# Eight PSUM banks dealt out anew in a two-layer hybrid block: separate rings for attention's maxima and scores, one bank for its value sums

## The chip, the cores and the metric

The kernel runs on one core of one Trainium2 chip, in one launch. The time is device microseconds; the time before is the median of three runs. A profile of one more execution, and its trace, stand beside it. A core has five engines that each run their own queue in order: TensorE (PE, matmuls; its weight loads are shown as PEld), VectorE (DVE), ScalarE (ACT), GpSimd (POOL) and SyncE (SP, which here issues nearly all DMAs). Matmuls write into PSUM; here all eight banks of 2 KB for each of the 128 partitions are given to the kernel's pools, and one bank holds one tile of 128 x 512 f32.

## The reference

Two layers over 1024 latent tokens and 256 context tokens, width 1024. In each layer a modulated rms norm feeds one wide input projection; its columns go to three branches, and their outputs are joined by an output projection that is added to the stream.

```python
for i in range(DEPTH):                                   # 2
    h, h_c = modulate(x, ...), modulate(ctx, ...)
    z, xbc, dtr, q, k, v, ga, ua, ub, gc = split_cols(h @ w_in[i])      # and for h_c
    ssd_lat  = ssd_branch(z, xbc, dtr, ...)              # conv of 5, chunked scan, 12 heads
    ql, kl   = rope(rmsnorm(q)), rope(rmsnorm(k))        # 12 query heads, 4 key heads, 64 wide
    attn_lat = attend(ql, concat(kl, kc), concat(vl, vc)) * silu(ga)    # softmax over 1280 keys
    conv_lat = conformer_branch(ua, ub, gc, ...)         # depthwise conv of 31, layernorm, matmul
    x = x + gate * (concat(ssd_lat, attn_lat, conv_lat) @ w_out[i])
    ...                                                  # the context likewise, in layer 0 only
return rmsnorm(x, final_norm_g)
```

## The kernel before, in words

All is f32. Products that need it are made of three fp32r matmuls on a split into a high and a low part (`mm3`). Each layer has three stages.

**Projections (`phase_b`).** For each of 10 tiles of 128 tokens, or for strips of 512 or 256 tokens, a group of 24 matmuls fills one PSUM tile of the pool `pm` (tag `m`); ACT or DVE reads it (`chain`, `gate`, `fm_fin`). Beside these groups DVE runs the depthwise convolutions (`conv_cm` into `cac`, `conv_x` into `xcv`), `conv_x` transposes its result on PE in three pieces of up to four tiles (`px`, `pt`, `px`; the copies are called `xsg`), and `cm_tail` transposes `cac` into a tile of `pt`, from which DVE takes the statistics and writes `xn`, which is transposed again into `px`.

**Attention (`attn`) with the scan (`ssd`) beside it.** A unit is a pair of query heads with 256 queries; there are 30 in layer 0 (24 large ones over 10 key tiles, 6 small ones over 2) and 24 large ones in layer 1. For a unit, `maxima` multiplies queries by keys in pieces of 512, 512 and 256 keys (12 matmuls, `m<-k_a,q_a` in the profile), DVE reduces each piece to a row maximum (`a_sm`, line 935), and the negated maxima go through a tile of `pv` into a row of the query operand. `scores` then makes for each key tile a transposed score tile (`m<-q_a,k_a` and `m<-q_b,k_b`), from which ACT takes the exponential (`a_p`), and DVE or POOL add the tiles up (`a_ac`, `a_a`). `values` multiplies `a_p` by the values into the first half of a tile of `pt` (`t<-a_p,vs`), in a block of four key tiles and one of six; `finish` puts the column sums into the second half of that tile (`t<-a_a,twos`), DVE takes their reciprocal (line 1011) and multiplies it by the first half (line 1012), and POOL applies the gate. Maxima run two units ahead of scores. The value block of a unit is emitted after the `finish` of the unit before it. `ssd` uses `px`.

**Output projection (`out_half`).** For each token tile and column half two groups (`pa`, `pb`) in `pm`, read by ACT and DVE.

The order on each engine is not written out by hand: `at(us)` gives what follows a due time, and a planner takes, of what is ready by its own estimate of durations and has a free PSUM or SBUF slot, what is due first. That order, and which tile gets which bank, is then fixed; on the chip every engine goes through its queue in order and waits where a bank is not yet read out. So a change of the pools can change the order everywhere.

The pools of PSUM before: `pm` 4 banks (all projection groups, maxima and scores), `pt` 2 (value accumulators, transposes, the modulation vectors of `ada`), `pv` 1 (transposes of queries and keys, the row of maxima, the small matmul of `cm_tail`), `px` 1.

Of the kernel before, what the change touches and what calls it, by code (L numbers as in the profile page):

```python
# [13 lines left out]
PSUM = bass.MemoryType.PSUM  # L14
DRAM = bass.MemoryType.DRAM

DEPTH = 2
PM = 4
PT_ = 2
PX_ = 1  # L20
CM_PACE = 1.7
TAIL = 40.0
# [138 lines left out]
def build(tc, a, out, depth=DEPTH, dump=None):  # L161
    nc = tc.nc
    es = ExitStack()
    V, S, G, P, Y = nc.vector, nc.scalar, nc.gpsimd, nc.tensor, nc.sync

    def at(us):
        tc.cur_priority = int(us * 100)

    def pool(st, name, bufs=1, **k):
        return st.enter_context(tc.tile_pool(name=name, bufs=bufs, **k))  # L170
# [3 lines left out]
    def mk(p, shape, tag, dt=F32, bufs=None):  # L174
        uid[0] += 1
        k = {} if bufs is None else {"bufs": bufs}
        return p.tile(shape, dt, tag=tag, name=f"{tag}_{uid[0]}", **k)

    cp = pool(es, "cp")
    dp = pool(es, "dp", space=DRAM)  # L180
    pm = pool(es, "pm", PM, space=PSUM)
    pt = pool(es, "pt", PT_, space=PSUM)
    pv_ = pool(es, "pv", 1, space=PSUM)
    px = pool(es, "px", PX_, space=PSUM)

    def dr(shape, name, dt=F32):
        t = dp.tile(shape, dt, tag=name, name=name)
        if dump is not None:
            dump[name] = t
        return t  # L190

    def mm(o, l, r, start, stop):
        P.matmul(o, l, r, start=start, stop=stop)  # L193

    def tr(o, i, idt):
        P.transpose(o, i, idt)  # L196

    def act(o, i, f, **k):
        S.activation(o, i, f, **k)  # L199
# [33 lines left out]
    for l in range(depth):  # L233
        t = mk(cp, [128, NCOL], f"colc{l}")
        Y.dma_start(out=t, in_=a["colc"][l])
        colc.append(t)
        t = mk(cp, [128, NROW], f"rowc{l}")
# [80 lines left out]
    def norm_tile(l, t, h, wp):  # L318
        r = 0 if t < 8 else 1
        xt = mk(wp, [128, DM], "n_x", bufs=3 if l == 0 else 1)  # L320
        if l == 0:
            Y.dma_start(out=xt, in_=a["xin"][t])
        else:
            for n in range(2):
                Y.dma_start(out=xt[:, 512 * n:512 * n + 512], in_=x_d[t][n])
        hh, hl = h
        tok = slice(t * 128, t * 128 + 128)
        hf = mk(wp, [128, KT, 128], "n_h", bufs=2 if l == 0 else 1)
        ss = mk(wp, [128, 4], "n_ss", bufs=4)
        act(hl[:, :, tok], xt.rearrange("p (k t) -> p k t", k=KT), AF.Square, accum_out=ss[:, 0:1])  # L330
        rs_pow(ss[:, 2:3], ss[:, 0:1], 1.0 / DM, ss[:, 1:2], 1)
        act(xt, xt, AF.Copy, scale=ss[:, 2:3])
        for f4 in range(2):
            ps = mk(*((pt, [128, 4, 128], "t") if f4 else (px, [128, 4, 128], "x")))
            for i in range(4):
                f = 4 * f4 + i
                tr(ps[:, i, :], xt[:, f * 128:(f + 1) * 128], idf)
            for i in range(4):
                f = 4 * f4 + i
                s1, s2 = msc[l][:, f, r:r + 1], msh[l][:, f, r:r + 1]  # L340
                if f4:
                    ts(V, hf[:, f, :], ps[:, i], s1, ALU.mult, s2, ALU.add)
                else:
                    act(hf[:, f, :], ps[:, i], AF.Identity, scale=s1, bias=s2)
        V.tensor_copy(hh[:, :, tok], hf)
        (V if t % 2 else G).tensor_tensor(hl[:, :, tok], hf, hh[:, :, tok].bitcast(F32), ALU.subtract)
# [87 lines left out]
    def phase_b(l, nh, b0, pp):  # L434
# [50 lines left out]

        def tm(i, n, j, t, w):
            nn = 280 if n == "q" and j == 2 else 256
            ps = mk(pm, [128, 512], "m")
            mm3(ps[:, 0:nn], lambda x, k: h[x][:, k, t * 128:t * 128 + 128], lambda x, k: w[x][:, k, :], KT)
            if n == "k":  # L490
                chain(ps, "k", t, k_d[t])
            elif n == "v":
                o = mk(qp, [128, 256], "c_v", bufs=2)
                act(o, ps[:, 0:256], AF.Copy)
                Y.dma_start(out=v_d[t], in_=o)
            else:
                if j == 2:
                    V.tensor_copy(dtr[:, t, :], ps[:, 256:280])
                if t < nq:
                    chain(ps, "q", t, q_d[j][t])  # L500
# [56 lines left out]
        def conv_x(j, t0):  # L557
            xp = xps[j]
            at(t0)
            o = mk(xp_p, [128, 1282], "xcv", bufs=2)  # L560
            w = sw[:, 5 * j:5 * j + 5]
            ts(V, o, xp[:, 0:1282], w[:, 0:1], ALU.mult, sw[:, 50 + j:51 + j], ALU.add)
            for k in range(1, 5):
                at(t0 + 2 * k)
                stt(o, xp[:, k:k + 1282], w[:, k:k + 1], o, ALU.mult, ALU.add)
            at(t0 + 10)
            th = mk(up_p, [128, 1282], "th")
            act(th, o, AF.Tanh)
            stt(o, th, 1.0, o, ALU.add, ALU.mult)
            if j >= 6:  # L570
                d = bT_d[j - 6] if j < 8 else cT_d[j - 8]
                Y.dma_start(out=d[:, 0:1024], in_=o[:, 0:1024])
                Y.dma_start(out=d[:, 1024:1280], in_=o[:, 1026:1282])
            if j < 8:
                at(t0 + XLAG)
                sg = mk(gp, [128, NT, 128], "xsg")
                for ta in (0, 4, 8):
                    n = min(4, NT - ta)
                    ps = mk(*((pt, [128, 4, 128], "t") if ta == 4 else (px, [128, 4, 128], "x")))
                    for t in range(ta, ta + n):  # L580
                        c0 = t * 128 + (2 if t >= 8 else 0)
                        tr(ps[:, t - ta, :], o[:, c0:c0 + 128], idf)
                    act(sg[:, ta:ta + n, :], ps[:, 0:n, :], AF.Copy)
                if j < 6:
                    d = xt_d[:, :, 128 * j:128 * j + 128]
                else:
                    d = bt_d[:, :, 128 * (j - 6):128 * (j - 6) + 128]
                Y.dma_start(out=d.rearrange("t p f -> p t f"), in_=sg)
# [34 lines left out]
        def block(i):  # L623
            u = FM_UNITS[i]
            u0 = b2 + 26 * i
            at(u0 - 20)
            w = wblock(wt, wt, a["wfm"][l, i], "wt", 2)
            tt = u0
            for m, (n, j) in enumerate(u):
                full = n == "xbc" or not last  # L630
                for t0, tn in ((0, 512), (512, 512), (1024, 256)):
                    if t0 >= 1024 and not full:
                        continue
                    at(tt)
                    ps = mk(pm, [128, 512], "m")
                    mm3(ps[:, 0:tn], lambda x, k: w[x][:, k, 128 * m:128 * m + 128],
                        lambda x, k: h[x][:, k, t0:t0 + tn], KT)
                    fm_fin(ps, n, j, t0, tn)
                    tt += 5.2 * tn / 512
                if n == "ua":  # L640
                    conv_cm(j, tt, CM_PACE)
                if n == "xbc":
                    conv_x(j, tt)
# [260 lines left out]
    def attn(l, ap, c0, pre):  # L904
# [18 lines left out]
        def maxima(i):  # L923
            qa, qb = qst[i]
            pcs = [(0, 512), (512, 512), (1024, 256)] if units[i][1] < 4 else [(1024, 256)]
            n = len(pcs)
            sm = mk(ap, [128, 4, 3], "a_sm", bufs=1)
            nm = mk(ap, [128, 4], "a_nm", F32R, bufs=2)
            for x in range(2):
                ka = kst[kv(i, x)][0].rearrange("p t k -> p (t k)")  # L930
                for t in range(2):
                    for j, (k0, kn) in enumerate(pcs):
                        ps = mk(pm, [128, 512], "m")
                        mm(ps[:, 0:kn], qa[:, x, t, :], ka[:, k0:k0 + kn], True, True)
                        V.tensor_reduce(sm[:, 2 * x + t, j:j + 1], ps[:, 0:kn], axis=AX.X, op=ALU.max)  # L935
                        yield
            V.tensor_reduce(nm, sm[:, :, 0:n], axis=AX.X, op=ALU.max, negate=True)
            ps = mk(pv_, [128, 4, 128], "v")
            for j in range(4):
                mm(ps[0:65, j, :], nm[:, j:j + 1].to_broadcast([128, 65]), idr, True, True)  # L940
            act(qb[64:65], ps[64:65].rearrange("p (x t) q -> p x t q", x=2), AF.Copy)
            yield
# [138 lines left out]
    def out_half(l, n, yp, wp, w, d0, fin):  # L1081
# [9 lines left out]
        for t in range(nq):  # L1091
# [12 lines left out]
            r = 0 if t < 8 else 1  # L1104
            xt = mk(yp, [128, 512], "ox", bufs=nb)
            Y.dma_start(out=xt, in_=a["xin"][t][:, s] if l == 0 else x_d[t][n])
            pa = mk(pm, [128, 512], "m")
            nk, k0, yy = pcs[0]
            mm3(pa, lambda x, k: yy[x][:, k, :], lambda x, k: w[k0 + k][x], nk)
            pb = mk(pm, [128, 512], "m")  # L1110
            for i, (nk, k0, yy) in enumerate(pcs[1:]):
                mm3(pb, lambda x, k: yy[x][:, k, :], lambda x, k: w[k0 + k][x], nk, i == 0, i == 1)
            t1 = mk(wp, [128, 512], "wor") if nb == 1 else mk(yp, [128, 512], "ot", bufs=2)
# [95 lines left out]
```

## Time and profile before

| | |
|---|---|
| median of 3 runs | 2922.65 us (2918.71 to 2924.61) |
| the profiled execution | 2926.13 us; its span, from the first to the last instruction, 2924.1 us |
| busy, share of the span | PE 2714.5 us (93%), PEld 2111.4 (72%), DVE 2175.7 (74%), ACT 1062.2 (36%), POOL 1165.6 (40%) |
| granted TensorE clock, mean | 0.965 |

In the groups of instructions a name such as `m<-k_a,q_a` says which tile is written from which. In rows of groups the figures are the number of instructions, the busy time in us and the mean of one in ns, and behind the bar the idle time of the engine just before them with what ended it. Rows of waits give the waiting engine and tile, what it waited for, us in total, how often, and the longest. Rows of the timeline give the start, the length, the engine and the instruction, with `x` for how many in a row are merged; a merged row's length runs over all of them.

### The profile page before, as it was taken

To read this page: it belongs to the slowest core of one execution; us is meant where nothing else is said; L and a number is where in the kernel's file an instruction comes from. 1 tells how busy PE (TensorE), PEld (TensorE's weight loads), DVE (VectorE), ACT (ScalarE), POOL (GpSimd) and SP (SyncE) were. 2 spreads that over 40 slices of the span, in tenths; PEclk is the share of its full clock that TensorE was granted. 3 is DMA by queue.
4 is the path that set the end of the run, shared out by engine and by line. 5 is a ranking of instruction groups with operands and counts; after the bars stand their busy time and mean duration, and the time that the engine had idled before them with its cause. 6 is when DMAs were issued, how large, how long until landed. Compare 5 with 4: busy or idle time off the path is not lost. (4 is left out here: it accounts for less than half of the span.)

```text
span 2924.1 us, 41057 instructions
## 1 busy us (share of the span) xinstructions
PE 2714.5 (93%) x15708; PEld 2111.4 (72%) x15708; DVE 2175.7 (74%) x2987; ACT 1062.2 (36%) x1801; POOL 1165.6 (40%) x832
## 2 busy tenths in 40 slices
PE   5999998999998888999999999999998998999998
PEld 3888876888856655666787998877886665666676
DVE  4476899973299989797445587999835989898644
ACT  4212221222245454454335222222224454644432
POOL 2244122232168677571112352222323667675111
PEclk9999998999999989899999999999999999999999
DMA  6551111223343222224645322113234232312554
GB/s 237 191 159 66 56 55 65 90 98 105 115 137 108 73 88 84 74 68 130 205 147 162 114 76 67 55 63 107 102 127 151 73 98 72 103 59 62 164 152 143
DMA packets 284035, 314.44 MB, mean 108 GB/s; under 512 B 27606, under 2 KB 219190, under 8 KB 282814
## 3 DMA queue, kind: packets, MB, share of 16 engines
q1 hardware_dynamic: 283838, 311.82, 33.5%
q8 instruction: 123, 2.02, 0.3%
q14 instruction: 74, 0.61, 0.1%
HBM read 236.25 MB, written 75.50 MB: 107 GB/s over the span
## 5 line engine op out<-in xcount | busy, mean ns | idle before, releaser
L193 PE MATMUL m<-hh,wth 128*128 128x512 f32 (+1 forms) x1440 | 533.7, 371 | 0.1
L193 PE MATMUL m<-hl,wth 128*128 128x512 f32 (+1 forms) x1440 | 532.2, 370 | 0.0
L193 PE MATMUL m<-hh,wtl 128*128 128x512 f32 (+1 forms) x1440 | 531.6, 369 | 0.0
L199 ACT ACTIVATE a_p<-m 128x512 f32<-128x512 f32 x492 | 285.5, 596 | 373.1 <-PE m L193 362.7
L208 DVE SCALAR_TENSOR_TENSOR cac<-up,cmw,cac 128x1295 f32<-128x1295 f32 (+1 forms) x240 | 383.2, 1617 | 1.9
L935 DVE TENSOR_REDUCE a_sm<-m 128x1 f32<-128x512 f32 (+1 forms) x600 | 331.0, 583 | 52.8 <-PE m L193 50.2
L359 POOL TENSOR_TENSOR wtl<-wr,wth 128x1024 fp32r<-128x1024 f32 x68 | 201.9, 2969 | 404.2 <-ACT wth L199 404.1
L193 PEld LDWEIGHTS m<-hh,wth 128*128 128x128 f32 x1440 | 273.0, 190 | 47.8 <-ACT th L199 0.5
L193 PEld LDWEIGHTS m<-hh,wtl 128*128 128x128 f32 x1440 | 272.5, 189 | 48.1
L193 PEld LDWEIGHTS m<-hl,wth 128*128 128x128 f32 x1440 | 272.7, 189 | 47.3
L193 PE MATMUL m<-q_a,k_a 128*128 128x512 f32 (+1 forms) x656 | 255.3, 399 | 23.1 <-ACT a_p L199 10.9
L193 PE MATMUL m<-k_a,q_a 128*128 128x512 f32 (+1 forms) x600 | 242.0, 440 | 24.9 <-DVE a_sm L935 19.3
L193 PE MATMUL t<-a_p,vs 128*64 128x256 f32 x1968 | 250.9, 397 | 0.9 <-ACT a_p L199 0.4
L193 PE MATMUL m<-woh,yl 128*128 128x512 f32 x576 | 227.7, 397 | 6.1 <-DVE yl L1101 5.9
L193 PE MATMUL m<-woh,yh 128*128 128x512 f32 x576 | 226.6, 396 | 5.2 <-ACT yh L199 5.2
L193 PE MATMUL m<-wol,yh 128*128 128x512 f32 x576 | 226.6, 395 | 0.8 <-DVE wol L1077 0.8
L193 PE MATMUL m<-q_b,k_b 65*128 65x512 f32 (+1 forms) x656 | 223.1, 350 | 0.0
L193 PEld LDWEIGHTS t<-a_p,vs 128*64 128x64 f32 x1968 | 138.7, 142 | 89.1 <-issue 17.2
L193 PEld LDWEIGHTS m<-q_a,k_a 128*128 128x128 f32 x656 | 129.3, 197 | 84.3 <-ACT a_p L199 23.4
L193 PEld LDWEIGHTS m<-k_a,q_a 128*128 128x128 f32 x600 | 117.0, 201 | 99.6 <-DVE a_sm L935 38.2
L199 ACT ACTIVATE wth<-wr 128x1024 fp32r<-128x1024 f32 (+1 forms) x84 | 89.3, 1063 | 255.6 <-DMA wr<-in_wfm 136.2
L193 PE MATMUL m<-wth,hh 128*128 128x256 f32 (+1 forms) x608 | 173.6, 288 | 1.3 <-ACT wth L199 0.8
(239 smaller groups left out, 5629.5 us busy)
## 6 DMA issues: line engine op xcount, KB each, us to landing
wr<-in_wfm SPq DMA_DIRECT2D x68, 512.0 KB, 3.6
s_cb<-cum_d SPq DMA_DIRECT2D x72, 384.0 KB, 3.7
ada_w<-in_adaw SPq DMA_DIRECT2D x32, 512.0 KB, 4.6
wor<-in_wout SPq DMA_DIRECT2D x64, 256.0 KB, 3.1
s_x<-xt_d SPq DMA_DIRECT2D x38, 384.0 KB, 3.2
yf<-ys_d SPq DMA_DIRECT2D x36, 384.0 KB, 3.9
yf<-ya_d SPq DMA_DIRECT2D x36, 384.0 KB, 4.2
yf<-yc_d SPq DMA_DIRECT2D x36, 256.0 KB, 2.9
```

The source lines that it names most:

```text
L193: P.matmul(o, l, r, start=start, stop=stop)
L199: S.activation(o, i, f, **k)
L208: V.scalar_tensor_tensor(o, i, s, i1, op0, op1)
L359: (e or G).tensor_tensor(lo[:, s], raw, hi[:, s].bitcast(F32), ALU.subtract)
L935: V.tensor_reduce(sm[:, 2 * x + t, j:j + 1], ps[:, 0:kn], axis=AX.X, op=ALU.max)
```

## The change

The eight banks are given out anew. `pm` has two banks and is used in attention by `scores` alone; a new pool `pn` (tag `n`) has three and is used in attention by `maxima`; the groups of the projections and of the output take the five in turn (`gemm`: n, n, m, n, m). `pt` has one bank instead of two, so a unit's value accumulator and the next unit's share it. In `norm_tile` the second half of the transposes goes to `pt` for odd tiles and to `pv` for even ones, and in `conv_x` the third piece goes to `pv` instead of to `px` again.

```diff
-PM = 4
-PT_ = 2
+PM = 2
+PN = 3
+PT_ = 1
...
     pm = pool(es, "pm", PM, space=PSUM)
+    pn = pool(es, "pn", PN, space=PSUM)
...
+    turn = [0]
+
+    def gemm():
+        turn[0] += 1
+        return mk(pm, [128, 512], "m") if turn[0] % 5 in (0, 3) else mk(pn, [128, 512], "n")
...                                          # norm_tile
-            ps = mk(*((pt, [128, 4, 128], "t") if f4 else (px, [128, 4, 128], "x")))
+            ps = mk(*((pt if t % 2 else pv_, [128, 4, 128], "t" if t % 2 else "v") if f4 else (px, [128, 4, 128], "x")))
...                                          # tm and block of phase_b, pa and pb of out_half
-            ps = mk(pm, [128, 512], "m")
+            ps = gemm()
...                                          # conv_x
-                    ps = mk(*((pt, [128, 4, 128], "t") if ta == 4 else (px, [128, 4, 128], "x")))
+                    ps = mk(*((pt, [128, 4, 128], "t") if ta == 4 else (px if ta == 0 else pv_, [128, 4, 128], "x" if ta == 0 else "v")))
...                                          # maxima
-                        ps = mk(pm, [128, 512], "m")
+                        ps = mk(pn, [128, 512], "n")
```

No instruction is added or left out: the same matmuls, reductions, copies and DMAs remain.

More of the change, by code (lines that the diff above doesn't have):

```diff
@@ L634, in block @@
                     at(tt)
-                    ps = mk(pm, [128, 512], "m")
+                    ps = gemm()
                     mm3(ps[:, 0:tn], lambda x, k: w[x][:, k, 128 * m:128 * m + 128],
@@ L932, in maxima @@
                     for j, (k0, kn) in enumerate(pcs):
-                        ps = mk(pm, [128, 512], "m")
+                        ps = mk(pn, [128, 512], "n")
                         mm(ps[:, 0:kn], qa[:, x, t, :], ka[:, k0:k0 + kn], True, True)
@@ L1106, in out_half @@
             Y.dma_start(out=xt, in_=a["xin"][t][:, s] if l == 0 else x_d[t][n])
-            pa = mk(pm, [128, 512], "m")
+            pa = gemm()
             nk, k0, yy = pcs[0]
             mm3(pa, lambda x, k: yy[x][:, k, :], lambda x, k: w[k0 + k][x], nk)
-            pb = mk(pm, [128, 512], "m")
+            pb = gemm()
             for i, (nk, k0, yy) in enumerate(pcs[1:]):
```

## The prediction

> **What bounds the kernel now.** I read the page's first lines, then the busy times by stage (the four stretches below are attention of layer 0 and of layer 1, then the projections of layer 0 and of layer 1), then PE's waits in each stretch.
>
> ```profile
> span 2924.1 us, 41057 instructions
> PE 2714.5 (93%) x15708; PEld 2111.4 (72%) x15708; DVE 2175.7 (74%) x2987; ACT 1062.2 (36%) x1801; POOL 1165.6 (40%) x832
> ...
> 820.00:1380.00 560.00, 504.41 (x3336) 342.16 (x3335) 493.71 (x683) 284.35 (x488) 359.31 (x216) 0.94 0.29 88
> 2225.00:2740.00 515.00, 471.13 (x3041) 317.82 (x3040) 452.03 (x636) 262.37 (x451) 316.95 (x189) 0.95 0.30 91
> 200.00:820.00 620.00, 587.29 (x3167) 500.86 (x3166) 454.45 (x492) 141.73 (x228) 170.59 (x137) 0.97 0.26 85
> 1700.00:2225.00 525.00, 507.80 (x2575) 426.19 (x2573) 406.23 (x459) 124.95 (x193) 151.25 (x121) 0.99 0.27 88
> ```
>
> Behind each stretch's length stand PE, PEld, DVE, ACT and POOL busy. PE bounds the whole: 2714.5 of 2924.1 us. In attention it shares that place with DVE (504.41 and 493.71 of 560 us, 471.13 and 452.03 of 515), and PE stands idle 55.6 and 43.9 us there, which is what this change can touch. In the projections PE idles 32.7 and 17.2 us.
>
> ```profile
> PE t L193 <- DVE a_a L981: 28.2, 17, 5.9
> PE m L193 <- DVE a_sm L935: 10.1, 13, 2.2
> PE m L193 <- ACT a_p L199: 5.3, 12, 1.9
> ...
> PE m L193 <- DVE a_sm L935: 17.4, 22, 2.2
> PE t L193 <- DVE a_a L981: 7.7, 11, 1.2
> PE m L193 <- ACT a_p L199: 6.6, 10, 2.4
> ...
> PE x L196 <- ACT xsg L199: 5.4, 2, 5.0
> ...
> PE t L280 <- DMA ada_w<-in_adaw: 19.1, 10, 13.7
> ```
>
> These are PE's waits in attention of layer 0, then of layer 1, then one row of the projections of layer 0 and one of the first 200 us. Waits of an `m` tile for `a_sm` (DVE) or `a_p` (ACT) are waits for a bank of the ring of four: 27.5 and 11.9 us. Waits for `a_a` are for data: the sums of `finish` wait until DVE has added the exponentials.
>
> **The change part by part.** No instruction goes or comes, so every term is a wait. The order on the queues is planned anew, which the trace of before cannot show; I bound each term by the order that stands, and by what a new order can hide.
>
> *Maxima and scores apart.* Whose tile waited for whose reader is read from the groups (layer 0, then layer 1):
>
> ```profile
> L193 PE MATMUL m<-q_a,k_a 128*128 128x512 f32 (+1 forms) x336 | 130.9, 400 | 10.5 <-DVE a_sm L935 5.5 <-ACT a_p L199 4.4
> L193 PE MATMUL m<-k_a,q_a 128*128 128x512 f32 (+1 forms) x293 | 116.7, 433 | 6.9 <-DVE a_sm L935 4.6 <-ACT a_p L199 0.9 <-ACT q_a L199 0.7
> ...
> L193 PE MATMUL m<-q_a,k_a 128*128 128x512 f32 (+1 forms) x320 | 124.4, 399 | 12.6 <-ACT a_p L199 6.6 <-DVE a_sm L935 5.1
> L193 PE MATMUL m<-k_a,q_a 128*128 128x512 f32 (+1 forms) x288 | 116.0, 438 | 14.4 <-DVE a_sm L935 12.3 <-ACT q_a L199 1.1
> ```
>
> A score tile (`m<-q_a,k_a`) can no longer wait for DVE's maxima: 5.5 + 5.1 = 10.6 us go, and with 0.9 us of maxima that waited for ACT, 11.5 us. This is the sure gain. Waits within a class can stay: maxima for `a_sm` 4.6 + 12.3 = 16.9 us, scores for `a_p` 4.4 + 6.6 = 11.0 us. At best they go too (27.9 us more).
>
> Against it: each class has fewer banks than the four that it could fill. In the order that stands, I compared each maxima matmul's start with the end of the reduction three tiles before, and each score tile's start with the end of the exponential two tiles before. The first and the last case of each kind:
>
> ```profile
> 807.63 0.69 DVE L935 TENSOR_REDUCE a_sm<-m 128x1 f32<-128x512 f32 x1 [0.16 <-PE m L193]
> 808.13 0.69 PE L193 MATMUL m<-k_a,q_a 128*128 128x512 f32 x1
> ...
> 2463.12 0.68 DVE L935 TENSOR_REDUCE a_sm<-m 128x1 f32<-128x512 f32 x1
> 2463.72 0.48 PE L193 MATMUL m<-k_a,q_a 128*128 128x512 f32 x1
> ...
> 866.31 0.60 ACT L199 ACTIVATE a_p<-m 128x512 f32<-128x512 f32 x1 [1.23 <-PE m L193]
> 866.69 0.40 PE L193 MATMUL m<-q_a,k_a 128*128 128x512 f32 x1
> ...
> 2723.97 0.60 ACT L199 ACTIVATE a_p<-m 128x512 f32<-128x512 f32 x1 [1.36 <-PE m L193]
> 2724.24 0.40 PE L193 MATMUL m<-q_a,k_a 128*128 128x512 f32 x1
> ```
>
> In the first pair the reduction ends at 808.32, 0.19 us after the matmul began; with three banks that matmul waits. Of 600 maxima 55 are so, by 43.0 us in all; of 492 score tiles 52, by 47.0 us. So the term lies between -27.9 (all waits within a class vanish) and +90.0 us (the order stays and nothing is taken up elsewhere). The planner knows of the two and three banks and will space the tiles by them, and a wait taken once shortens the next; nine tiles in ten fit already. I take +8, near the low middle, because the 27.9 us that are paid today for the same kind of wait with four shared banks are the nearest row, and the new rings are a little tighter for each class.
>
> *Value accumulators in one bank.* The next unit's first value block may start only when DVE has multiplied by the reciprocal. Today it starts earlier:
>
> ```profile
> 842.57 0.65 PE L193 MATMUL t<-a_a,twos 128*64 128x256 f32 x4
> 843.34 1.75 DVE L1011 RECIPROCAL a_rc<-t 128x256 f32<-128x256 f32 x1
> 845.23 1.95 PE L193 MATMUL t<-a_p,vs 128*64 128x256 f32 x16
> 846.61 0.41 DVE L1012 TENSOR_TENSOR a_rc<-t,a_rc 128x256 f32<-128x256 f32 x1
> ...
> 2721.32 0.87 PE L193 MATMUL t<-a_p,vs 128*64 128x256 f32 x6
> 2724.80 0.65 PE L193 MATMUL t<-a_a,twos 128*64 128x256 f32 x4
> 2729.69 0.42 DVE L1012 TENSOR_TENSOR a_rc<-t,a_rc 128x256 f32<-128x256 f32 x1
> ```
>
> In the first pair the bank would come free at 847.02 and the block began at 845.23: 1.79 us too early. Of the 52 units that follow another one in their layer, 41 began too early, by 118.3 us in all (median 1.8). The last is the second one shown: the unit's first values at 2721.32, before the sums of the unit ahead, whose product ends at 2730.11, 8.8 us later; the small units have this too. 118.3 us is the upper end. Nothing need be lost if the planner puts other work into the gap: the six score tiles and maxima that follow in the unit are independent of this bank, and the `a_p` ring of five pairs holds a whole unit, so scores can run on. What is queued behind a wait is PE's whole queue, and through it DVE's reductions and ACT's exponentials; the block itself is not urgent, since the unit's second block comes some 10 us later. The lower end is therefore 0. But the planner's estimate has to fit the chip: the nearest row for "PE placed behind a DVE result that comes late" is that of the sums for `a_a`, 28.2 + 7.7 = 35.9 us over 54 finishes, 0.66 us each. The new wait follows the old one by 2.16 us of reciprocal and product (1.75 + 0.41) and what DVE puts between, and PE has just been brought level with DVE there, so I take half of that, +18 us.
>
> [...]
>
> *`conv_x`'s third piece in `pv`.* It no longer waits for ACT's copy out of `px`: the 5.4 us of the row above go, in a stage where PE bounds. -5.4 (between -5.4 and 0, if `pv` or DVE's `xcv` is late instead).
>
> *`cm_tail` with one bank.*
>
> ```profile
> 2084.21 0.60 PE L196 MATMUL t<-msk,cac 128*128 128x128 f32 x4
> 2085.77 0.80 DVE L205 TENSOR_SCALAR xn<-t,bs 128x512 f32<-128x512 f32 x1
> ...
> 600.00:700.00 100.00, 97.56 (x526) 83.07 (x525) 52.98 (x108) 26.18 (x42) 35.02 (x26) 1.00 0.33 111
> 2050.00:2150.00 100.00, 98.74 (x458) 80.50 (x457) 65.78 (x101) 25.51 (x37) 35.29 (x24) 1.00 0.33 111
> ```
>
> Here the transposes of the next tile start 2.36 us before the tile before is read out; they would move behind it. What covers this is the groups of the projections, which fill PE to 98 and 99 of 100 us in those stretches (last two rows). I take 0; without that cover 16 such pairs would cost about 16 x 2.36 = 38 us. `ada` with one bank is bound by its weights (19.1 us of waits for DMA above): 0. `norm_tile` keeps two banks in turn: 0. Five banks for the projection groups instead of four: no row of PE waiting for a reader of a group's tile in those stages is above 1 us, so 0.
>
> *Sum.* -11.5 + 8 + 18 - 5.4 = +9.1 us on the profiled execution (2926.13 us; span 2924.1), which lies 3.5 us (0.12%) above the median. Put on the median: 2931.8 us, +0.3%.
>
> **The rivals.**
>
> *It gains (ends on the other side).* One mechanism: the planner finds cover between the sums and the next value block. The point that decides is whether PE's work between them lasts longer than DVE's way from the sums to the product (4.45 us in the first case shown, 842.57 to 847.02; 5.31 in the second, 2724.80 to 2730.11). Then the +18 falls away, the 11.5 + 5.4 us go, and with the narrower rings at 0 the time is 2905.8; with the 27.9 us as well, 2877.9. For it: 11 of the 52 blocks start after the product already, by up to 7.5 us. Against it: 41 do not, and all that PE can take into the gap are maxima and scores whose rings are narrower now.
>
> *Nothing to be seen.* Attention is held by DVE as much as by PE: a wait that PE loses in front of a score tile it finds again at the next maximum, since DVE's 493.71 us of work in 560 stay. Then the terms cancel: 2917 to 2928.
>
> *The read-out lies bare.* The order stays nearly as it is, and the 118.3 us are paid: 2922.65 + 118.3 + 8 - 16.9 = 3032.1. For it: 41 of 52. Against it: the planner sees the single bank, and 29 of the 41 are under 3 us (44 us together), which a few score tiles fill. [...]
>
> **How the numbers follow.** Less than 0.2% (5.8 us) cannot be told from no change here. Chances: a small loss as summed 0.35, bare read-out 0.10 (slower together 0.45), gain 0.37, nothing 0.18. The likeliest single sign is slower, so 2932 is given; its own range is 2928.5 to 2965. The range for 8 in 10 goes from 2890 (part of the waits within a class gone as well) to 2988 (about half of the bare read-out's 118.3 us beside the other terms: 2922.65 + 59 + 8 - 1.9, the `xsg` wait and most of the 11.5 us not saved).
>
> **What would show it.** Right: waits of value matmuls for the product (`a_rc`, line 1012) appear on PE, some 0.3 us a unit; no score tile waits for `a_sm`; both attention stretches are longer by some 5 us each; the wait for `xsg` is gone. Wrong: value matmuls start behind the product without a wait, and PE's idle time in attention falls below 99.5 us; or the change sits outside attention, for instance in the projections through another order.

## The result, and the profile after

The changed kernel takes 2950.97 us (median of 6 runs, 2945.18 to 2952.93) against 2924.91 us for the one before, measured beside it: 1.0087 of its time, 95% interval 1.0073 to 1.0101. It is slower by 26 us. The direction was forecast, and the time lies in the range; the mechanism on which the forecast rested is not the one that costs. The profiled execution took 2950.16 us.

The first two lines of the page:

```profile
span 2948.3 us, 41078 instructions
PE 2719.0 (92%) x15708; PEld 2111.6 (72%) x15708; DVE 2176.6 (74%) x2987; ACT 1059.2 (36%) x1801; POOL 1187.4 (40%) x832
```

The engines' own work is the same in number; the 21 instructions more (41057 before) are semaphore instructions. PE does the same 15708 matmuls in 4.5 us more, and stands idle 229.3 us instead of 209.6. Where, is read from six stretches: up to the first reduction of attention, attention of layer 0 to its last reciprocal product, from there to the end of the output projection, up to attention of layer 1, attention, the rest. First before, then after; behind the length stand PE, PEld, DVE, ACT, POOL busy, and then the granted clock.

```profile
0.00:804.20 804.20, 741.53 (x4330) 620.61 (x4331) 552.36 (x750) 198.47 (x341) 223.69 (x202) 0.97 0.33 112
804.20:1384.90 580.70, 521.49 (x3396) 353.18 (x3396) 511.90 (x714) 296.62 (x508) 370.02 (x223) 0.93 0.31 94
1384.90:1615.50 230.60, 219.60 (x973) 176.78 (x972) 112.53 (x166) 92.99 (x150) 40.55 (x33) 0.99 0.56 171
1615.50:2228.60 613.10, 593.66 (x3260) 510.69 (x3259) 460.03 (x594) 149.44 (x243) 189.78 (x164) 0.98 0.28 91
2228.60:2744.40 515.80, 472.11 (x3049) 318.38 (x3048) 454.44 (x640) 264.44 (x453) 314.25 (x187) 0.95 0.29 90
2744.40:2924.10 179.70, 166.12 (x709) 131.77 (x707) 84.47 (x126) 60.28 (x107) 27.29 (x25) 0.98 0.51 155
```

```profile
0.00:801.60 801.60, 741.48 (x4332) 622.89 (x4333) 558.11 (x750) 198.62 (x341) 230.07 (x202) 0.97 0.34 113
801.60:1370.30 568.70, 503.86 (x3329) 339.89 (x3328) 493.36 (x694) 280.47 (x486) 375.37 (x222) 0.93 0.28 85
1370.30:1633.30 263.00, 241.44 (x1053) 190.18 (x1054) 127.42 (x185) 107.75 (x172) 41.70 (x33) 0.97 0.57 174
1633.30:2252.50 619.20, 595.50 (x3243) 512.10 (x3243) 453.58 (x595) 149.00 (x243) 197.20 (x164) 0.98 0.28 90
2252.50:2737.80 485.30, 450.06 (x2987) 300.04 (x2986) 445.75 (x619) 248.56 (x431) 315.94 (x187) 0.98 0.26 80
2737.80:2948.30 210.50, 186.63 (x768) 146.55 (x768) 98.36 (x146) 74.78 (x128) 27.10 (x26) 0.93 0.56 165
```

Both attention stretches are shorter, by 12.0 and 30.5 us. That is not a gain as it stands: PE ran 67 and 62 matmuls fewer in them, and the stretches behind are longer by 32.4 and 30.8 us. Before, 65 and 60 matmuls of the output projection began ahead of attention's end; after, none does. Only idle time (length less PE busy) can be compared. It goes from 59.2 to 64.8 us and from 43.7 to 35.2 in attention, together -2.8; behind attention from 11.0 to 21.6 and from 13.6 to 23.9, together +20.9; in the two stretches of projections -2.6 and +4.3. Of the 24.2 us by which the span is longer, 20.9 are idle time at the seam between attention and output projection, in both layers.

What happens at the seam is read from SyncE's queue: gates (`gt`) and weights (`wor`) of the output projection, before and after.

```profile
1343.30 0.80 SPq L1090 DMA_DIRECT2D gt<-gt_d  x2
1344.14 0.90 SPq L1075 DMA_DIRECT2D wor<-in_wout  x2
...
2697.39 0.32 SPq L1090 DMA_DIRECT2D gt<-gt_d  x1
```

```profile
1364.79 0.80 SPq L1098 DMA_DIRECT2D gt<-gt_d  x2
1365.63 0.91 SPq L1083 DMA_DIRECT2D wor<-in_wout  x2
...
2738.34 0.32 SPq L1098 DMA_DIRECT2D gt<-gt_d  x1
```

These tiles lie in the SBUF of the scan (`sr.close()` in `layer`), and the first `gt` is issued within 0.2 us of the scan's last instruction in both kernels. Before, that was 42 and 47 us ahead of attention's end; after, 5.5 us ahead and 0.5 us behind. So the output groups that ran under attention's end no longer can. Both ends moved: counted from the start of attention, the scan ends 24.1 and 17.1 us later than before, and attention, without those output matmuls, ends 12.0 and 30.5 us earlier. PE after its last sums in layer 0, and ACT, which splits the first weights:

```profile
1366.86 1.09 PE L201 MATMUL t<-a_a,twos 128*64 128x256 f32 x4
1374.37 0.77 PE L201 MATMUL n<-woh,yh 128*128 128x512 f32 x1 [6.42 <-issue]
1374.93 0.63 PE L201 MATMUL n<-wol,yh 128*128 128x512 f32 x1
1375.36 0.76 PE L201 MATMUL n<-woh,yl 128*128 128x512 f32 x1
...
1378.05 0.40 PE L201 MATMUL n<-woh,yl 128*128 128x512 f32 x1
1378.29 0.40 PE L201 MATMUL n<-woh,yh 128*128 128x512 f32 x1
...
1371.16 1.15 ACT L207 ACTIVATE woh<-wor 128x512 fp32r<-128x512 f32 x2 [10.17 <-DMA wor<-in_wout]
```

PE is idle for 6.42 us, and then the matmuls start 0.43 us apart (1374.93, 1375.36), from 1378.05 on 0.24 us; the granted clock is 0.50 from 1371.2 to 1378.0. For 3.7 us behind the idling (1374.37 to 1378.05) the matmuls thus come at nearly twice the later spacing. Before, the first output matmul came at 1364.24, 20.7 us ahead of attention's end.

PE's waits in attention, layer 0 and then layer 1:

```profile
PE t L201 <- DVE a_a L989: 23.3, 11, 5.0
PE n L201 <- DVE a_sm L943: 11.3, 14, 2.6
PE m L201 <- ACT a_p L207: 7.0, 15, 1.4
PE t L201 <- DVE a_rc L1020: 3.0, 1, 3.0
...
PE n L201 <- DVE a_sm L943: 8.5, 14, 1.7
PE t L201 <- DVE a_a L989: 8.1, 7, 2.9
PE m L201 <- ACT a_p L207: 2.2, 8, 0.5
```

For a bank, maxima (`n`) wait for DVE alone and scores (`m`) for ACT alone, as said. Of the wait on which the forecast was built, value matmuls for the product (`a_rc`), there is one, of 3.0 us. All 52 value blocks that follow another unit now start behind the product, by 0.06 to 13.8 us; with one bank they must, and PE, but for that one wait, had other work in the meantime.

### The profile page after: what moved, and what is told of

The parts are those of the page before. It is cut to its first block, busy times and chain, and to the rows that moved or that the text cites. A ratio compares the mean times of both kernels' runs of the same rounds, so it can differ in the third digit from the quotient of the medians.

```text
span 2948.3 us, 41078 instructions
## 1 busy us (share of the span) xinstructions
PE 2719.0 (92%) x15708; PEld 2111.6 (72%) x15708; DVE 2176.6 (74%) x2987; ACT 1059.2 (36%) x1801; POOL 1187.4 (40%) x832
## 5 line engine op out<-in xcount | busy, mean ns | idle before, releaser
L943 DVE TENSOR_REDUCE a_sm<-n 128x1 f32<-128x512 f32 (+1 forms) x600 | 325.9, 580 | 33.4 <-PE n L201 31.2
L201 PE MATMUL n<-hh,wth 128*128 128x512 f32 (+1 forms) x872 | 319.9, 367 | 5.3 <-ACT th L207 5.3
L201 PE MATMUL n<-hl,wth 128*128 128x512 f32 (+1 forms) x872 | 318.5, 365 | 0.0
L201 PE MATMUL n<-hh,wtl 128*128 128x512 f32 (+1 forms) x872 | 318.4, 365 | 0.0
L201 PE MATMUL n<-k_a,q_a 128*128 128x512 f32 (+1 forms) x600 | 221.0, 420 | 27.6 <-DVE a_sm L943 24.0
L201 PE MATMUL m<-hh,wth 128*128 128x512 f32 (+1 forms) x568 | 215.5, 379 | 8.8 <-ACT th L207 8.8
L201 PE MATMUL m<-hh,wtl 128*128 128x512 f32 (+1 forms) x568 | 214.3, 377 | 0.0
L201 PE MATMUL m<-hl,wth 128*128 128x512 f32 (+1 forms) x568 | 214.2, 377 | 0.0
L201 PEld LDWEIGHTS n<-hh,wth 128*128 128x128 f32 x872 | 166.2, 191 | 33.0 <-ACT th L207 5.5
L201 PEld LDWEIGHTS n<-hl,wth 128*128 128x128 f32 x872 | 166.1, 190 | 27.5
```

## The experiments

Theory A: the scan now ends too late against attention's end, so its SBUF comes free too late and the output weights lose their cover. Rivals: R, the prediction's bank waits; B, the new pools themselves keep output groups from running beside attention; C, the loss is spread over the whole order.

For all runs: idle time of PE in both attention stretches and behind them to the end of the output projections, and when the first `gt` is issued against attention's end (layer 0, layer 1), from the profiled executions. Times are medians, and each ratio is to runs of the kernel before beside it (medians 2924.7 to 2928.4 us). e3 and e4 leave out work, so their times compare with each other alone.

| kernel | time, us | ratio to before (95%) | idle in attention | idle behind | `gt` against attention's end |
|---|---|---|---|---|---|
| before | 2924.9 | 1 | 102.9 | 24.6 | -42, -47 |
| after | 2951.0 | 1.0087 (1.0073 to 1.0101) | 100.1 | 45.5 | -5, +1 |
| e1 | 2946.3 | 1.0076 (1.0060 to 1.0092) | 90.5 | 71.8 | +3, +12 |
| e2 | 2991.4 | 1.0232 (1.0214 to 1.0251) | 129.8 | 20.8 | -112, -102 |
| e3 | 2880.5 | 0.9848 (0.9833 to 0.9863) | 61.3 | 35.8 | -29, -2 |
| e4 | 2881.2 | 0.9855 (0.9826 to 0.9885) | 80.3 | 23.4 | -58, -78 |
| f1 | 2946.0 | 1.0061 (1.0045 to 1.0077) | 106.4 | 27.9 | -35, -51 |
| f2 | 2971.4 | 1.0140 (1.0111 to 1.0168) | 115.9 | 26.4 | -173, -135 |
| f3 | 2965.5 | 1.0135 (1.0109 to 1.0161) | 102.4 | 82.7 | +3, +23 |
| f4 | 2944.4 | 1.0059 (1.0038 to 1.0080) | 99.2 | 45.7 | -22, +7 |
| g1 | 2937.0 | 1.0039 (1.0025 to 1.0054) | 100.2 | 32.3 | -20, +1 |
| g2 | 2930.0 | 1.0012 (1.0001 to 1.0024) | 106.7 | 27.4 | -43, -33 |
| g3 | 2937.4 | 1.0037 (1.0023 to 1.0051) | 99.1 | 56.5 | +3, +12 |
| h1 | 2928.9 | 1.0002 (0.9986 to 1.0019) | 106.7 | 27.1 | -45, -47 |

Taken by layer, these 14 kernels give 28 seams. Wherever `gt` is issued 20 us or more ahead of attention's end (17 seams), PE idles 10.1 to 15.6 us behind attention; wherever it comes less than 6 us ahead or later (11 seams), 18.7 to 44.1 us. Within e3, f4 and g1 layer 0 is of the first kind (10.5, 13.8, 13.7 us) and layer 1 of the second (25.3, 31.9, 18.7). In layer 0 of e1, f3 and g3 the scan ends later still than its `gt`: 8.6, 12.9 and 22.7 us behind attention.

**e1: one part alone, the value bank; its spare bank goes to the shared ring.**

```diff
-PM = 4
-PT_ = 2
+PM = 5
+PT_ = 1
```

> The kernel before with one part of the change alone: the value accumulators in one bank, the shared ring of maxima, scores and projection groups with five banks instead of four. Theory A (the loss of the change lies at the seam, where the output weights wait for the scan's SBUF, and the scan ends late because attention now takes more of the engines): the single bank makes attention shorter or leaves it, because in the changed kernel 50 of 52 value blocks start behind the product without a wait; expected 2915 to 2945 us, with the start of the output loads later by the same amount as the scan's end. Rival R (the prediction's: the bank itself costs waits of value matmuls): 2940 to 2960 us, with PE waiting for line 1012 in most units.

```profile
802.50:1348.90 546.40, 494.59 (x3281) 340.21 (x3282) 490.48 (x689) 280.13 (x485) 369.12 (x221) 0.94 0.29 86
1348.90:1623.50 274.60, 238.79 (x1092) 192.59 (x1088) 130.77 (x190) 109.36 (x173) 41.63 (x35) 0.94 0.56 172
2241.90:2719.90 478.00, 439.35 (x2921) 299.24 (x2921) 445.24 (x616) 250.66 (x430) 320.69 (x185) 0.96 0.27 81
2719.90:2941.90 222.00, 186.03 (x842) 149.72 (x836) 100.63 (x150) 76.17 (x129) 27.75 (x27) 0.92 0.52 157
...
PE m L193 <- DVE wol L1077: 24.6, 2, 24.4
```

2946.3 us, no ring split, and the same picture in a stronger form: attention idles least of all kernels that leave nothing out (51.8 + 38.7 us), and behind it PE idles 35.8 and 36.0 us, 24.4 of them in one wait for the split output weights (last line). The time lies in R's range and 1.3 us above A's. But R's waits are not there: PE waits for line 1012 eight times, 5.9 us in all. The place speaks for A.

**e2: the other part alone, rings of their own, two value banks.**

```diff
-PN = 3
-PT_ = 1
+PN = 2
+PT_ = 2
...
-        return mk(pm, [128, 512], "m") if turn[0] % 5 in (0, 3) else mk(pn, [128, 512], "n")
+        return mk(pm, [128, 512], "m") if turn[0] % 2 else mk(pn, [128, 512], "n")
```

> The changed kernel with the other part alone: rings of their own for maxima and scores, two banks each, and two banks for the value accumulators as before. Theory A: if the separate rings are what makes attention shorter, attention is shorter than before by 10 to 40 us over both layers here too, and the seam costs as much or more, 2930 to 2955 us. Rival R (narrow rings cost waits, 43 us for three banks and more for two): attention longer than before, 2950 to 2990 us.

```profile
806.90:1427.70 620.80, 548.61 (x3438) 364.40 (x3438) 505.06 (x723) 298.51 (x513) 366.65 (x223) 0.92 0.30 91
2263.10:2821.70 558.60, 501.00 (x3079) 333.43 (x3078) 452.63 (x646) 263.18 (x458) 309.07 (x188) 0.92 0.29 86
```

2991.4 us, 1.4 us above R's range, with attention longer by 40.1 and 42.8 us. Four banks cut in two and two cost attention 26.9 us of idling against the four shared ones; the waits of maxima for `a_sm` and of scores for `a_p` add up to 53.6 us, against 27.9 before. Here R is right: rings of two and two cost. The seam is not hurt, since the scan ends 112 and 102 us ahead of attention.

**e3 and e4: the scan shortened by leaving out the line below, in the changed kernel and in the one before.**

```diff
-                        G.tensor_tensor(e, e, cm[:, d, g].unsqueeze(1).to_broadcast([128, 6, 128]), ALU.mult)
```

> The changed kernel with the scan shortened: the multiplication of the decay matrix by the masked product (four POOL instructions of 2.3 us in each of 18 chunks) is left out. Theory A: the scan ends some 80 us earlier in each layer, the output weights are loaded under attention, and the changed kernel no longer loses: 2850 to 2890 us, below the kernel before with the same part left out by 10 to 40 us. Theory B (the seam comes from the new pools, because the output groups find no bank beside attention): still slower than its partner by about 25 us.

> The kernel before with the same multiplication of the scan left out, as the partner of the run ahead. Theory A: 2880 to 2915 us, with the scan ending before attention by 50 us or more, and slower than the changed kernel with the same part left out by 10 to 40 us. Theory B: faster than that one by about 25 us.

2880.5 and 2881.2 us: the difference of 26 us is gone (the four runs of e4 spread over 18 us), so it hangs on the scan and not on the pools as such. B falls, the more so as in layer 0 of e3 the first output matmul starts 17.3 us ahead of attention's end with the new pools. But the changed kernel does not come out ahead, as A had it: its scan still ends only 29 and 2 us before attention does, and of the 19.0 us that attention gains (61.3 against 80.3 us idle) 12.4 go again behind it (35.8 against 23.4), all of it in layer 1 (25.3 against 10.1).

**f1: the value bank alone, no other bank given out.**

```diff
-PT_ = 2
+PT_ = 1
```

> The kernel before with one value bank and nothing else: the shared ring stays at four banks, one bank of the eight is unused. Theory A1 (the single value bank makes the planner run scores and maxima ahead instead of value blocks, and so shortens attention at the scan's expense): attention of layer 0 is at most 560 us long (580.7 before, 546.3 with a fifth shared bank), the scan ends later, and the time is 2935 to 2960 us. Theory A2 (the fifth shared bank did it): attention of layer 0 is 575 us or longer, 2925 to 2965 us.

```profile
0.00:813.00 813.00, 744.61 (x4331) 621.94 (x4332) 554.90 (x751) 198.34 (x341) 227.60 (x202) 0.96 0.34 111
813.00:1395.10 582.10, 523.47 (x3382) 355.30 (x3380) 508.01 (x710) 294.13 (x501) 366.96 (x222) 0.92 0.31 93
2250.20:2762.40 512.20, 464.36 (x3040) 315.58 (x3039) 456.81 (x642) 262.78 (x453) 315.59 (x187) 0.96 0.30 91
```

A2, as far as attention goes: with one value bank it is as long as before (582.1 and 512.2 us) and idles 3.5 us more. It is the fifth shared bank that shortens it: e1 differs from f1 in that alone, and idles 15.9 us less in attention, while its scan ends behind attention instead of 35 and 51 us ahead. That f1 is 18 us slower than before has other places: of the 20.0 us by which its span is longer, 8.8 lie in the first stretch (813.0 us instead of 804.2), and 3.5 are idling in attention. In that stretch `pt` also serves `norm_tile` and `conv_x`, which the change spreads over `pv`, and the changed kernel's first stretch is 801.6; that this is the reason was not tested.

**f2: the spare bank to the scan** (`PT_ = 1`, `PX_ = 2`, the shared ring four).

> The kernel before with the second value bank given to the scan's pool (px two banks, pt one, the shared ring four). Theory A (the lateness of the scan is what costs): if the scan's single bank is part of its lateness (POOL waited 72.8 and 36.2 us for PE's x tiles before), the scan ends 10 us or more earlier relative to attention's end than in the changed kernel and the time is 2880 to 2925 us. If the scan is held by POOL's own work, it ends as late as with one bank: 2935 to 2960 us.

2971.4 us, outside both ranges. The scan's bank does hold it up: with two banks the scan ends 173 and 135 us ahead of attention's end. But that does not pay: attention idles 9.5 us more than in f1, and PE is busy 2738.6 us in all instead of 2719.8. An early end of the scan gives a short seam (26.4 us idle behind attention), and in these runs a lead beyond some 20 us shortened it no further.

**f3 and f4: two of the scan's additions per chunk moved from POOL to DVE**, in e1 and in the changed kernel.

```diff
-                    G.tensor_tensor(yo, yo, tm, ALU.add)
+                    V.tensor_tensor(yo, yo, tm, ALU.add)
```

> One value bank and five shared banks (as in e1), and two of the scan's POOL additions of each chunk (s_yo, line 806 of the kernel before, 2.1 us each) moved to DVE. Theory A: the scan ends some 10 to 30 us earlier in each layer, the output weights come earlier, 2905 to 2935 us against 2946 for e1. Theory B (the scan's end does not matter, the pools do): 2940 to 2960 us.

> The changed kernel with the same two additions of the scan moved from POOL to DVE. Theory A: the scan ends 10 to 30 us earlier in each layer, 2910 to 2940 us against 2951. Theory B: 2945 to 2965 us, since DVE, which is nearly full in attention, gets more work.

f3 missed: the scan ended later, not earlier, and 2965.5 us lies above both ranges and is worse than e1. The edit did not do what it was for, so f3 tells nothing for B. f4, 2944.4 us, lies between its two ranges; the edit brought the scan's end forward in layer 0 (`gt` 22 us ahead, 13.8 us of idling behind attention instead of 21.6) and failed in layer 1 (7 us behind, 31.9 instead of 23.9).

**g1, g2, g3: six of sixteen pairs of output weights freed from the scan's end**, in the changed kernel, the one before, and e1. The scan's backward states get a pool of their own, and the weights of the first group take over their slots one after the other.

```diff
-            ho = mk(sp, [128, 768], f"hb{c - 1}")
+            if c == 8:
+                ho = mk(sp, [128, 768], "hb7")
+            else:
...                                          # two states to one tile of the new pool ep
-        for k in [12, 13, 14, 15] + list(range(12)):
+        for k in list(range(6)) * (ep is not None) + [12, 13, 14, 15] + list(range(6 if ep is not None else 0, 12)):
+            if ep is not None and k < 6:
+                at(t0 - 40 + k * 0.5)
...                                          # hi and lo of these six are taken from ep
-            r = mk(wp, [128, 512], "wor", bufs=2 if n == 0 else 1)
+            r = mk(wp if ep is None else ep, [128, 512], "wor", bufs=2 if n == 0 else 1)
```

> The changed kernel with six of the sixteen pairs of output weights of each layer's first half (those of the scan's own output, which the first group uses) loaded earlier: their SBUF is that of the scan's backward states, in a pool of its own, so that they wait for single states and no longer for the end of the scan; they are due 40 units earlier. Nothing is left out. Theory A' (the loss is PE standing between attention's end and the output groups, since all output weights wait for the scan's SBUF; idle after attention is 21.6 and 23.9 us against 11.0 and 13.6 before, and the first output matmuls then run at half rate): first output matmul within 6 us of attention's end or before it, idle behind attention 10 us less over both layers, 2925 to 2943 us. Theory C (the loss is spread over the order of everything, the seam is only where it shows): 2945 to 2960 us.

> The kernel before with the same early weights, as a partner. Its output weights already came 41 to 47 us before attention's end, and its first output matmul 19 to 21 us before it. Theory A': little to gain, 2915 to 2930 us, so that the changed kernel gains more from it. Theory C: both change alike.

> One value bank and a shared ring of five (e1, the shortest attention of all, 546 and 478 us, with 35.8 and 36.0 us of PE idle behind it) with the same early weights. Theory A': gains most, 15 to 40 us: 2905 to 2930 us. Theory C: 2940 to 2955 us.

```profile
800.10:1386.10 586.00, 520.63 (x3368) 351.85 (x3368) 508.78 (x711) 291.24 (x504) 373.00 (x223) 0.92 0.31 92
1386.10:1626.50 240.40, 226.75 (x1016) 182.46 (x1015) 112.45 (x168) 95.79 (x154) 39.62 (x32) 0.99 0.56 167
2244.90:2735.90 491.00, 456.25 (x2987) 303.60 (x2986) 450.85 (x625) 252.01 (x437) 317.38 (x187) 0.97 0.27 83
2735.90:2935.10 199.20, 180.52 (x768) 144.56 (x768) 91.84 (x140) 70.27 (x122) 25.85 (x26) 0.96 0.55 164
```

The lines are of g1: behind attention PE idles 13.7 and 18.7 us, together 13.2 us less than in the changed kernel, and its profiled span is shorter by just that (2948.3 to 2935.1); attention idles as much as there (100.2 us). The medians give 14 us of the 26. The same edit brings nothing in the kernel before (1.0012), so C's "both change alike" did not come. So the seam is a cause, and g1 takes back about half of the loss. Not all of that is shown to come from the early weights: in layer 0 attention's stretch also became 17.3 us longer, and `gt` came 20 us ahead of its end; f4 idles as little there (13.8 us) with that lead and no early weights. In layer 1, with `gt` as late as in the changed kernel, the gain is 5.2 us (23.9 to 18.7), and the first output matmul still comes 8.6 us behind attention, later than A' had it. g3, 2937.4 us, gained 9 us against e1, less than expected, and lies between its two ranges: its scan ends 22.7 and 11.6 us behind attention, and its first output matmul starts 32.5 and 20.3 us behind; what holds it there was not taken apart. None of the versions that leave nothing out beats the kernel before.

**h1: the third piece of `conv_x` alone** (the line of the change, on the kernel before).

> The kernel before with one line of the change alone: the third piece of conv_x's transposes goes to pv instead of waiting for px. The prediction's term: the 5.4 us that PE waited for the copy (xsg) go, and nothing else moves: 2917 to 2923 us, 0.9975 to 0.9990 of the time before. Rival (a new order elsewhere eats it, as it did in the larger changes): 2923 to 2935 us, although the wait for xsg is gone.

PE's waits from 200 to 800 us, before and then in h1:

```profile
PE x L196 <- DVE xcv L208: 12.8, 2, 10.6
PE x L196 <- ACT xsg L199: 5.4, 2, 5.0
PE t L196 <- DVE xcv L208: 4.2, 1, 4.2
PE t L196 <- DVE cac L208: 2.4, 1, 2.4
...
PE x L196 <- DVE xcv L208: 18.3, 3, 10.3
PE t L196 <- DVE cac L208: 4.3, 1, 4.3
PE t L196 <- DVE xcv L208: 3.9, 1, 3.9
```

The wait for `xsg` is gone, and the next transposes wait for `xcv`, the result of DVE's convolution, instead: 5.5 us more in `px` and 1.9 for `cac`. No gain (1.0002), the rival's case.

## Why the prediction was right or wrong

**Slower, +9 us:** right in sign, too small (+26), and for another reason. The terms that made it a loss did not come as priced, and the loss that came was in no term, so the sign was luck. The prediction's own list of what would show it wrong names what happened: value blocks behind the product without a wait, and a change that sits outside attention. The sum, term by term:

- *Waits across the classes, -11.5 us:* right as to the waits: no score waits for DVE's maxima and no maximum for `a_p` in the lines above. That 11.5 us were saved is not shown; all idling in attention together fell by 2.8 us.
- *Narrower rings, +8 us:* too large for three and two banks. Waits within the classes were 27.9 us and are 29.0 (11.3 + 7.0 + 8.5 + 2.2), +1.1. With two and two banks they are 53.6 (e2).
- *One value bank, +18 us:* this step failed. It took the `a_a` wait as the model for a new wait. The trace has 3.0 us of it, and f1 3.5 us of idling in attention for the single bank; that f1 as a whole is 18 us slower agrees with the term by chance, since most of that lies outside attention. The 118.3 us of blocks that "began too early" told only that the planner had no reason to wait; given one, it put other work there. The point that was named as deciding, cover between sums and block, decided that way, but the rival built on it forecast a gain, which did not come. The bare read-out, the rival that would have cost 118.3 us, did not occur: in this kernel the next block could be ordered later.
- *`conv_x`, -5.4 us:* not paid in h1, where it stands alone, and for the reason that the term's own bracket named: DVE's `xcv` is late instead, since the transposes that follow wait for it.
- *Five banks for the projection groups, 0:* did not hold. In the changed kernel groups wait for a bank that ACT reads late (`th` is read out of a group's tile), 5.3 us in layer 0 and 8.8 in layer 1; before, no such row is in the list. In layer 1 this and `cac` (+4.0) outweigh the 11.7 us of waits for `xcv` that are gone, and the projections there idle 4.3 us more. That the split into two and three banks causes the new waits was not tested. PE's waits in the projections, after (layer 0; layer 1), then before (layer 1):

```profile
PE n L201 <- ACT th L207: 5.3, 1, 5.3
...
PE m L201 <- ACT th L207: 8.8, 2, 7.7
PE t L204 <- DVE cac L216: 5.3, 1, 5.3
...
PE t L196 <- DVE xcv L208: 11.7, 3, 6.1
...
PE t L196 <- DVE cac L208: 1.3, 1, 1.3
```

- *`cm_tail`, `norm_tile`, `ada` at 0:* the first stretch idles 2.6 us less; what of the change does that was not taken apart.
- *What the sum lacked:* the seam, +20.9 us of idling. The prediction said that the order is planned anew and priced nothing outside the waits on banks. The row for it was in the trace of before: the gates' load at 1343.30 and the output weights' at 1344.14, right behind the scan's last instruction and 42 us ahead of attention's end. That lead went when the scan ended later and attention earlier; no wait on the changed banks shows it.

**"Attention longer by some 5 us each":** wrong; shorter by 12.0 and 30.5 us, by matmuls moved out. In idle time it is 5.6 us more in layer 0 and 8.5 less in layer 1. **"Nothing to be seen", since DVE holds attention:** wrong too: the fifth bank alone took 15.9 us of idling out of attention (f1 to e1).

What stays open: why, with the banks given out anew, the scan falls back against attention. That it does is shown by f1 and e1; its reasons are not. Of POOL, which runs many of the scan's steps, the trace shows this much: in layer 0, 176 instructions in nearly the same groups take 442.0 us (914 to 1356) instead of 431.0 (906 to 1337), and its waits for attention's product (`a_g` for `a_rc`) are 15.9 us instead of 7.6. Nor is it settled what makes up the rest of the loss beyond the 13 to 14 us that g1 recovers; in g1 the loads of the other ten pairs still come behind the scan's end.

## What to carry to other kernels

Where a stage's buffers overlay those of another chain, look up how far that chain ends ahead of the stage that covers its loads: this lead is a resource, and a change that lets the chain end later or the covering stage end earlier spends it. When an order is planned anew, "this instruction would have started too early" bounds little beyond the old order; price also what hangs on other chains, such as memory that comes free late. And compare stages by idle time of the bounding engine, not by length: here attention got 42 us shorter and the kernel 26 us slower.

## What the runs showed of the hardware that was not expected

At the seam of the changed kernel the granted clock is low, and not only while PE stands idle. Behind attention it is 0.50 from 1371.2 to 1378.0 and from 1381.5 to 1391.7 in layer 0, and for 23.9 us from 2740.0 on in layer 1, where PE stands idle for 11.59 us before the first output matmul; PE is busy for 22.5 us of these stretches. In the kernel before the granted clock is 1.00 over the first 15 and nearly 20 us behind attention.

PE's busy time for the same 15708 matmuls is not constant: 2698.8 us in e1, 2714.5 before, 2719.0 after and 2754.1 in e2 (first lines of the pages). The granted clock over the whole run does not put them in this order (0.958, 0.965, 0.964, 0.955), and the ends of matmuls are modelled in the profile, so the cause stays open.
